# Order of work at the ends of the FFN passes, of banks and of side sums in a one-core Mamba-2 / Conformer trunk

## The chip, the cores and the metric

The kernel runs on one core of a Trainium2 chip. Its time is the device time of one launch in microseconds (us). Five engines run their own queues side by side: TensorE (PE in the profile, its weight loads PEld), VectorE (DVE), ScalarE (ACT), GpSimd (POOL) and SyncE (SP), which issues the loads and stores. An engine takes its instructions in the order of its queue and waits on semaphores for what others produce.

## The reference

A trunk of two residual layers over a sequence of 1024 rows, width D = 1024, float32:

```python
for i in range(DEPTH):                      # DEPTH = 2
    if i == 0: h = h + mamba2_mixer(rmsnorm(h, ssm_norm), ...)
    else:      h = h + conformer_conv_module(rmsnorm(h, cv_norm), ...)
    h = h + (silu(u @ w_gate) * (u @ w_up)) @ w_down      # u = rmsnorm(h, ffn_norm[i]), D_FF = 2816
return rmsnorm(h, final_norm)
```

The mixer is a Mamba-2 layer (input projection, a convolution of 4 taps, a chunked scan over 32 heads, gated norm, output projection). The Conformer module is a product to 2048 columns (pw1) with a sigmoid gate, a causal depthwise convolution of 31 taps, a layer norm over D with silu, and a product back to 1024 columns (pw2).

## The kernel before

Everything is held transposed: features on the 128 partitions, sequence along the free axis, in two blocks of T = 512 columns (block 0 and block 1). h is kept in eight tiles of 128x512 per block. D_FF is 22 tiles of 128 features.

*Products.* Each float32 operand is split into a high and a low part: ScalarE makes the high one (L210), VectorE or GpSimd subtracts to get the low one (L211). `gemm` (L231) then issues three matmuls per pair, low weights first (wlo with uhi, whi with ulo, whi with uhi), all on line L235. A product over D is thus 24 matmuls of 128x512. What a norm yields is called u: `norm_u` multiplies h by the inverse root (L321, tile `un` or `ru`), and splits it into `uhi` and `ulo`.

*FFN.* `ffn` yields, for a part of so many tiles, gate and up products (hidden tiles `hid`), and eight down products `dn`, one per tile of h, with three matmuls per hidden tile of the part: a part of six tiles has 18 matmuls per down product, one of two has 6. After each down product VectorE adds it to h (L870); in the last part of a pass it also adds the square of h to a running sum `ssum` for the next norm (`sq_add`, L256). `rstd_a` splits that sum into `sumh` and `suml`; `rstd_b` sums it over the partitions with two matmuls against ones (L282), and forms the inverse root with ScalarE (L286) and three passes of VectorE in PSUM (L287 to L289). Most gate and up products go through `seven` instead: two tiles of features at once, with both halves of the block, by seven products of half-size operands (matmuls of 128x256, L766) in place of eight. It needs sums of weights (`ws`, `wh`) and sums of u, made by `sums_u`: two `join`s per four feature tiles put uhi + ulo back into a buffer `ru` (L684), then differences (L696 to L698, L704) and splits into `tu`. All of these are 128x1024 passes on VectorE.

*The order.* `run` builds one list of units; `put` and `at` slide side work into places of that list (negative places count from its end). Each engine's queue follows this list, with priorities: the convolution (`conv31`, 8 x 31 VectorE passes, L980) has its priority put back, so that VectorE takes it up where it has nothing else. `chain` and `chain7` string the parts of a pass together; in `chain7` the down products of a part are mixed in among the next part's products, `hold` of them are held back, and those of the last part come at the end. The sequence from the first FFN on is: FFN0 of block 0; the Conformer module of block 0, into which 14 of the 22 tiles of FFN0 of block 1 are woven (their gate and up products stand ahead of pw1 and beside the convolution, their down products cover the layer norm); the other 8 tiles of FFN0 of block 1; the Conformer module of block 1, with 14 tiles of FFN1 of block 0; the other 8 of these; FFN1 of block 1 with the final norm.

*Buffers.* `Slots` gives out named SBUF buffers, longest free first. PSUM has eight banks, given out in turn by `bank`; each new phase (`banks`) begins its turn at the first of its list. A product waits until its bank's last reader is done: for a gate product this is ScalarE's silu (`sg_s`, L834), then VectorE's product with the up half (L835).

*Start.* `selects` (L170) makes two constants for the scan, a selector `sel` and a mask `part`, with fills and affine selections on GpSimd, and one sum on VectorE (L186). It is in the list behind the first norm.

*End.* `final` makes the last norm, in one unit for eight multiplications (L1066) with their stores.

Of the kernel before, what the change touches and what calls it, by code (L numbers as in the profile page):

```python
# [14 lines left out]
P = 128  # L15
# [33 lines left out]
class Slots:  # L49
# [5 lines left out]

    def new(self, name, dt=F32):
        assert self.free, [x[2] for x in self.own.values()]
        i = self.free.popleft()
        self.cnt += 1
        t = self.pool.tile(self.shape, dt, tag=f"{self.prefix}{i}", name=f"{name}_{self.prefix}{self.cnt}")  # L60
        self.own[id(t)] = (i, t, name)
        return t
# [42 lines left out]
class Trunk:  # L105
    def __init__(self, ctx, tc, io):
        self.tc, self.nc, self.io = tc, tc.nc, io
        self.cp = ctx.enter_context(tc.tile_pool(name="cp", bufs=1))
        self.wp = ctx.enter_context(tc.tile_pool(name="wp", bufs=1))
        self.ps = ctx.enter_context(tc.tile_pool(name="ps", bufs=1, space=PSUM))  # L110
        self.banks(mm=(0, 1, 2, 3), ss=(4, 5, 6, 7))
# [25 lines left out]
    def consts(self):  # L137
# [30 lines left out]
        nc.vector.tensor_copy(self.gtr, gt)  # L168
        self.small.drop(tmp)
    def selects(self):  # L170
        nc = self.nc


        tmp = [self.small.new("selo"), self.small.new("selp")]
        nc.gpsimd.memset(self.part, 1.0)
        for k, t in enumerate(tmp):
            selo = t.rearrange("h (q c) -> h q c", c=64)
            nc.gpsimd.memset(t, 1.0)
            for g in range(NG):
                s = selo[32 * g:32 * g + 16]  # L180
                nc.gpsimd.affine_select(out=s, in_=s, pattern=[[1, 8], [0, 64]], compare_op=ALU.is_equal,
                                        fill=0.0, base=8 * k, channel_multiplier=-1)
                m = self.part[32 * g:32 * g + 16, k:k + 1]
                nc.gpsimd.affine_select(out=m, in_=m, pattern=[[0, 1]], compare_op=ALU.is_ge,
                                        fill=0.0, base=-8 * k + 7 * (1 - k), channel_multiplier=2 * k - 1)
        nc.vector.tensor_tensor(self.sel, tmp[0].rearrange("h (q c) -> h q c", c=64),  # L186
                                tmp[1].rearrange("h (q c) -> h q c", c=64), ALU.add)
        self.small.drop(*tmp)
    def halves(self):
# [478 lines left out]

    def sums_u(self, b):

# [8 lines left out]
        def join(q):  # L679
            if q == 0:  # L680
                self.RU[b] = [self.big.new("ru"), self.big.new("ru")]
            h, l = self.UB[b][2 * q:2 * q + 2]
            for j in (slice(0, 2), slice(2, 4)):
                tt(self.RU[b][q][:, j], f32(h[:, j]), f32(l[:, j]), ALU.add)  # L684
# [367 lines left out]
    def final(self, b, part=()):  # L1052
# [8 lines left out]

        def second():
            bc = self.rstd_b(st["x"], D, w=n)
            for d in range(KD):
                h = self.hv(b)[d][:, t0:t0 + n]
                nc.vector.scalar_tensor_tensor(h, h, self.pcol("final", d), bc, op0=ALU.mult, op1=ALU.mult)  # L1066
                nc.sync.dma_start(self.io["yT"][d, :, b * T + t0:b * T + t0 + n], h)
        return [Unit(first), Unit(second)]


    def run(self):
# [20 lines left out]
        dt[0].load = early[0].load = None  # L1092
        q = dt[:1] + nu + early + [call(lambda: self.big.drop(*rb))] + [call(self.selects)] + dt[1:] + ip[:NR]
        q += [call(lambda: self.small.drop(fac))] + ip[NR:]
# [31 lines left out]
        q += cv[4:] + put(c[2:], *at(ln, (-10, -9, -8, -6, -4, -3, -2, -1)))  # L1126
# [4 lines left out]
        q += [call(self.phase7)] + put(c, *at(n0, (-13, -11, -9, -7, -5))) + [call(self.phase, 8)]  # L1131
# [3 lines left out]
        q += put(c[:2], *at(n1, (0, 1))) + [call(self.phase, 6, nc.gpsimd)]  # L1135
# [3 lines left out]
        q += cv[4:] + put(c[2:], *at(ln, (-10, -9, -8, -6, -4, -3, -2, -1)))  # L1139
        q += [call(self.phase, 8)]  # L1140
        self.whole = {1}
        q += put(p2, *at(self.sums_u(0), (2, 3, 4, 5, 6)))
# [110 lines left out]
```

## Time and profile before

| | us |
|---|---|
| median of 3 runs | 2559.18 (2556.84 to 2560.3) |
| the profiled execution, its own time | 2561.22 |
| its span in the trace | 2559.3 |
| TensorE busy | 2502.3 (98%) |
| VectorE busy | 2050.1 (80%) |
| ScalarE busy | 1281.8 (50%) |
| GpSimd busy | 490.6 (19%) |

The span goes from the first to the last instruction; 1.9 us of the launch lie around it. A busy share of a whole span says little about a stage, so the profile is read by windows: for a stretch of time each row gives the busy time of each engine, the count of its instructions in brackets, and PEclk, the mean clock granted to TensorE as a share of full speed.

### The profile page before, as it was taken

How to read it: one execution, taken by the hardware profiler on the slowest of the kernel's cores; microseconds unless marked ns; L12 is line 12 of the kernel's file. 1: busy time of each engine (PE TensorE's matmuls, PEld its weight loads, DVE VectorE, ACT ScalarE, POOL GpSimd, SP SyncE). 2: the span in 40 equal slices, each digit the busy share in tenths (PEclk: the TensorE clock that was granted, in tenths of full speed). 3: DMA queues.
4: the chain of work that ended last, by engine and by line, in shares of the span. 5: the costliest groups of instructions: out<-in, count | busy, mean ns of one | idle time of the engine just before them, and what ended most of it. 6: DMA issues, size and time to landing. Idle time of an engine off the chain costs nothing.

```text
span 2559.3 us, 35509 instructions
## 1 busy us (share of the span) xinstructions
PE 2502.3 (98%) x13570; PEld 2117.2 (83%) x13570; DVE 2050.1 (80%) x2991; ACT 1281.8 (50%) x2284; POOL 490.6 (19%) x466
## 2 busy tenths in 40 slices
PE   8999999999999999997999999989999999999998
PEld 5888787887887799996888889968888899799997
DVE  7888989888888886767899677579996776996675
ACT  5665575666566454444332365352323654554443
POOL 4213312112111000000444530004444300000000
PEclk9999999999999999998999999999999999999999
DMA  4222222222223232222323232222233322332322
GB/s 138 83 71 79 75 63 80 74 78 78 76 70 103 79 122 93 98 73 66 99 94 96 91 132 95 71 75 98 94 97 96 127 99 77 126 122 93 110 89 71
DMA packets 72314, 233.51 MB, mean 91 GB/s; under 512 B 8016, under 2 KB 14416, under 8 KB 65232
## 3 DMA queue, kind: packets, MB, share of 16 engines
q1 hardware_dynamic: 72144, 231.25, 27.9%
q8 instruction: 106, 1.74, 0.3%
q14 instruction: 64, 0.52, 0.1%
HBM read 227.02 MB, written 4.19 MB: 90 GB/s over the span
## 4 chain that ended last, share of the span: by engine, by line
PE 92%; DVE 5%; ACT 1%; DMA 1%; issue 1%; POOL 1%; SPq 0%; DVEq 0%; ACTq 0%; POOLq 0%
PE p L235 65%; PE p L766 21%; PE p L603 1%; PE p L607 1%; DVE wlo L211 1%; PE p L595 1%; PE p L570 1%; PE p L558 1%; DMA wst<-w_dn 1%; PE p L571 1%; DVE h L1066 0%; DVE un_s L321 0%; PE p L586 0%; ACT whi L210 0%; PE p L282 0%
## 5 line engine op out<-in xcount | busy, mean ns | idle before, releaser
L210 ACT ACTIVATE whi<-wst 128x512 fp32r<-128x512 f32 (+3 forms) x676 | 402.7, 597 | 750.4 <-PE p L235 614.2
L235 PE MATMUL p<-uhi_b,wlo 128*128 128x512 f32 x1432 | 574.6, 402 | 20.0 <-ACT sg_s L834 15.1
L235 PE MATMUL p<-ulo_b,whi 128*128 128x512 f32 x1432 | 565.8, 395 | 5.6 <-POOL ulo_b L211 5.5
L235 PE MATMUL p<-uhi_b,whi 128*128 128x512 f32 x1432 | 565.2, 395 | 0.0
L211 POOL TENSOR_TENSOR wlo<-wst,whi 128x512 fp32r<-128x512 f32 x232 | 302.0, 1303 | 775.2 <-ACT whi L210 775.2
L235 PE MATMUL p<-hid_b,whi 128*128 128x512 f32 x1344 | 421.8, 395 | 0.0
L211 DVE TENSOR_TENSOR wlo<-wst,whi 128x512 fp32r<-128x512 f32 (+2 forms) x444 | 306.3, 692 | 141.3 <-ACT whi L210 138.4
L235 PEld LDWEIGHTS p<-uhi_b,wlo 128*128 128x128 f32 x1432 | 271.0, 189 | 87.2 <-ACT sg_s L834 16.1
L235 PEld LDWEIGHTS p<-ulo_b,whi 128*128 128x128 f32 x1432 | 271.0, 189 | 70.6 <-POOL ulo_b L211 7.5
L766 PE MATMUL p<-uhi_b,wh_b 128*128 128x256 f32 x1728 | 322.6, 282 | 1.6 <-ACT uhi_b L210 1.2
L235 PEld LDWEIGHTS p<-uhi_b,whi 128*128 128x128 f32 x1432 | 270.9, 189 | 62.5 <-issue 0.3
L235 PEld LDWEIGHTS p<-hid_b,whi 128*128 128x128 f32 x1344 | 254.1, 189 | 55.6 <-DVE hid_b L211 0.2
L766 PEld LDWEIGHTS p<-uhi_b,wh_b 128*128 128x128 f32 x1728 | 272.6, 189 | 4.3 <-ACT uhi_b L210 1.4
L235 PE MATMUL p<-hid_b,wlo 128*128 128x512 f32 x672 | 266.9, 398 | 6.9 <-DVE h L870 5.2
L766 PE MATMUL p<-ulo_b,wh_b 128*128 128x256 f32 x864 | 243.4, 282 | 0.8 <-DVE ulo_b L211 0.8
L766 PE MATMUL p<-tu_b,wh_b 128*128 128x256 f32 x1296 | 171.4, 282 | 0.0
L766 PEld LDWEIGHTS p<-ulo_b,wh_b 128*128 128x128 f32 x864 | 163.8, 190 | 2.9 <-DVE ulo_b L211 1.0
L766 PEld LDWEIGHTS p<-tu_b,wh_b 128*128 128x128 f32 x1296 | 162.3, 190 | 0.9
L980 DVE SCALAR_TENSOR_TENSOR p<-ci_b,par,p 128x503 f32<-128x503 f32 (+28 forms) x240 | 160.1, 734 | 0.6
L982 DVE SCALAR_TENSOR_TENSOR p<-ci_b,par,p 128x512 f32<-128x512 f32 x232 | 158.7, 750 | 0.5
L210 ACT ACTIVATE wh_b<-ws_b 128x1024 fp32r<-128x1024 f32 x108 | 113.8, 1058 | 86.4 <-PE p L766 35.3
L235 PEld LDWEIGHTS p<-hid_b,wlo 128*128 128x128 f32 x672 | 127.1, 189 | 35.8 <-DVE h L870 7.0
(239 smaller groups left out, 3966.6 us busy)
## 6 DMA issues: line engine op xcount, KB each, us to landing
wq_b<-w_gu SPq DMA_DIRECT2D x54, 1024.0 KB, 4.8
wst<-w_in SPq DMA_DIRECT2D x80, 512.0 KB, 3.5
wst<-w_gu SPq DMA_DIRECT2D x68, 512.0 KB, 3.5
wst<-w_pw SPq DMA_DIRECT2D x48, 512.0 KB, 3.5
wst<-w_dn SPq DMA_DIRECT2D x48, 384.0 KB, 3.2
wst<-w_out SPq DMA_DIRECT2D x64, 256.0 KB, 2.6
wst<-w_dn SPq DMA_DIRECT2D x32, 448.0 KB, 3.3
wst<-w_dn SPq DMA_DIRECT2D x32, 256.0 KB, 2.7
```

What stands on the lines that cost most here:

```text
L210: self.nc.scalar.activation(hi, src, AF.Copy)
L211: (eng or self.nc.vector).tensor_tensor(lo, src, hi.bitcast(F32), ALU.subtract)
L235: self.nc.tensor.matmul(acc, a, b, start=n == 0, stop=n == tot - 1)
L558: nc.tensor.transpose(xt[:, zs(j)], self.XS[i][:, j, zs(z)], self.ident)
L570: nc.tensor.matmul(sg, self.gtr, aml, start=True, stop=False)
L571: nc.tensor.matmul(sg, self.gtr, amh, start=False, stop=True)
L595: nc.tensor.matmul(O[:, zs(j)], H[:, zs(j)], CT[:, zs(z)], start=True, stop=True)
L603: nc.tensor.matmul(Y[po:po + 64, zs(hh // 2)], self.XDT[z % 2][:, hh * 64:(hh + 1) * 64], E[:, zs(r)], start=True, stop=True)
L607: nc.tensor.matmul(S, self.BTOK[:, zs(z)], self.XDD[z % 2], start=True, stop=True)
L766: nc.tensor.matmul(to, x, y, start=n == 0 and not more, stop=n == 11, skip_group_check=True)
L980: nc.vector.scalar_tensor_tensor(acc[:, s:], x[:, HALO:TW - s], w(s), acc[:, s:], op0=ALU.mult, op1=ALU.add)
L982: nc.vector.scalar_tensor_tensor(acc if s < 30 else c, x[:, HALO - s:TW - s], w(s), acc, op0=ALU.mult, op1=ALU.add)
```

## The change

Six edits, all of order, buffers or of who makes a constant; the matmuls and their operands stay what they are.

1. **Parts.** FFN0 of block 0 has parts of 6, 6 and 6 tiles behind the four that the mixer's end has done (6, 6, 4 and 2 before). The pieces of 8 tiles in FFN0's and FFN1's other calls of `chain7` are 2 then 6 (6 then 2 before). `hold` is 0 there, and the other block's norm stands at other places.
2. **Four products ahead.** Of the gate and up products that are woven into a Conformer stage, four stand ahead of pw1 (two before), with the norm's second half behind the first of them; correspondingly two fewer come later.
3. **Banks by age.** A new phase begins its turn at the bank that was taken longest ago.
4. **Selector.** `selects` forms both constants from the identity with eight small VectorE operations, and is called among the first things of the program. GpSimd's 16 selections and 3 fills are gone.
5. **Sums of u.** In the two stages that overlap pw2, `sums_u` takes the buffers that were freed last, not those longest free.
6. **Final scaling.** `final` gives its eight multiplications in four units of two.

```diff
-    def new(self, name, dt=F32):
+    def new(self, name, dt=F32, last=False):
-        i = self.free.popleft()
+        i = self.free.pop() if last else self.free.popleft()
...
     def banks(self, **use):
-        self.use, self.turn = use, dict.fromkeys(use, 0)
+        self.use, self.turn = use, {}
+        for k, b in use.items():
+            self.turn[k] = min(range(len(b)), key=lambda i: self.taken[b[i]], default=0)
     def bank(self, tag):
...
         self.turn[tag] += 1
+        self.count += 1
+        self.taken[i] = self.count
...
     def selects(self):
-        nc.gpsimd.memset(self.part, 1.0)
-        for k, t in enumerate(tmp):
...
+        tt(rows, idg(0), idg(1), ALU.add)
+        tt(rows, rows, idg(2), ALU.add)
+        tt(rows, rows, idg(3), ALU.add)
+        tt(one[:, 0], rows[:, 0], rows[:, 1], ALU.add)
+        for w in (4, 2):
+            tt(rows[:, :, :w], rows[:, :, :w], rows[:, :, w:2 * w], ALU.add)
+        tt(self.part.unsqueeze(2), rows[:, :, 0:1], rows[:, :, 1:2], ALU.add)
+        nc.vector.tensor_copy(self.sel, one[:, 0].unsqueeze(2).to_broadcast([P, 8, 64]))
...
-    def sums_u(self, b):
+    def sums_u(self, b, late=False):
-                self.RU[b] = [self.big.new("ru"), self.big.new("ru")]
+                self.RU[b] = [self.big.new("ru", last=late) for _ in range(2)]
...
-        return [Unit(first), Unit(second)]
+        return [Unit(first)] + [Unit(lambda d=d: second(d)) for d in range(0, KD, 2)]
...
     def run(self):
         self.consts()
+        self.selects()
...
-        c = self.chain7(fast(0, 0, 6, [0]), fast(0, 6, 6, [0]), fast(0, 12, 4, [0]), fast(0, 16, 2, [0], [0]), free=0, hold=5)
-        q += [call(self.phase7)] + put(c, *at(n1, (-11, -9, -7, -5, -3))) + [call(self.phase, 8)]
+        c = self.chain7(fast(0, 0, 6, [0]), fast(0, 6, 6, [0]), fast(0, 12, 6, [0], [0]), free=0, hold=0)
+        q += [call(self.phase7)] + put(c, *at(n1, (-10, -8, -7, -6, -5))) + [call(self.phase, 8)]
...
-        q += put(c[:2], *at(n0, (0, 1))) + [call(self.phase, 6, nc.gpsimd)]
+        q += put(c[:4], *at(n0, (0, 1))) + [call(self.phase, 6, nc.gpsimd)]
...
-        q += put(p2, *at(self.sums_u(1), (2, 3, 4, 5, 6)))
+        q += put(p2, *at(self.sums_u(1, True), (2, 3, 4, 5, 6)))
-        c = self.chain7(fast(0, 0, 6, [1]), fast(0, 6, 2, [1], [1]), free=1, hold=6)
+        c = self.chain7(fast(0, 0, 2, [1]), fast(0, 2, 6, [1], [1]), free=1, hold=0)
...
-        c = self.chain7(fast(1, 14, 6, [0]), fast(1, 20, 2, [0], [0]), free=0, hold=5)
-        q += [call(self.phase7)] + put(c, *at(n1, (-13, -11, -9, -7, -5)))
+        c = self.chain7(fast(1, 14, 2, [0]), fast(1, 16, 6, [0], [0]), free=0, hold=0)
+        q += [call(self.phase7)] + put(c, *at(n1, (-10, -8, -7, -6, -5)))
...
-        q += put(c, *at(self.sums_u(1), (1, 2, 4)), (2, f0[:1]), (3, f0[1:]), (-7, f1[:1]), (-5, f1[1:])) + f2
+        q += put(c, *at(self.sums_u(1), (1, 2, 4)), (2, f0[:1]), (3, f0[1:]), *at(f1, (-7, -5, -4, -3, -2))) + f2
```

Helper lines stand lower in the new file by six or seven: L235 is L241, L211 is L217, L282 is L288, L684 is L691, L766 is L773, L870 is L877, L980 is L987, L1066 is L1075.

How the queues change is seen in three places. The first is TensorE's queue behind the mixer, where four gate and up products follow each other (p_1007, p_1013 and p_1017 are their accumulators, given out in that order, wlo and whi the parts of their weights). Before:

```order
L235 MATMUL p_1007_7430<-ulo_b_7075,whi_7369 128x512
L235 MATMUL p_1007_7430<-uhi_b_7074,whi_7369 128x512
L235 MATMUL p_1017_7502<-uhi_b_6951,wlo_7464 128x512
L235 MATMUL p_1017_7502<-ulo_b_6952,whi_7463 128x512
L235 MATMUL p_1017_7502<-uhi_b_6951,whi_7463 128x512
...
L235 MATMUL p_1013_7471<-uhi_b_6951,wlo_7423 128x512
L235 MATMUL p_1013_7471<-ulo_b_6952,whi_7422 128x512
```

Now:

```order
L241 MATMUL p_1007_7417<-ulo_b_7062,whi_7356 128x512
L241 MATMUL p_1007_7417<-uhi_b_7061,whi_7356 128x512
L241 MATMUL p_1013_7458<-uhi_b_6938,wlo_7410 128x512
L241 MATMUL p_1013_7458<-ulo_b_6939,whi_7409 128x512
L241 MATMUL p_1013_7458<-uhi_b_6938,whi_7409 128x512
...
L241 MATMUL p_1017_7489<-uhi_b_6938,wlo_7451 128x512
L241 MATMUL p_1017_7489<-ulo_b_6939,whi_7450 128x512
```

Nine matmuls of p_1017 stood ahead of p_1013; now p_1013 goes whole ahead of p_1017.

The second is TensorE's queue at the end of FFN0 of block 0: down products (hid), gate and up products of the other block (uhi, ulo), the norm's two matmuls (suml, sumh) and the first of pw1, which reads the u of that norm. Before:

```order
L235 MATMUL p_1286_10661<-hid_b_10556,wlo_10620 128x512
L235 MATMUL p_1286_10661<-hid_b_10556,whi_10619 128x512 x2
...
L235 MATMUL p_1322_10835<-uhi_b_10631,wlo_10803 128x512
...
L235 MATMUL p_1329_10914<-uhi_b_10631,wlo_10824 128x512
...
L282 MATMUL p_1328_10870<-suml_s_10832,onesr 128x512
L282 MATMUL p_1328_10870<-sumh_s_10831,onesr 128x512
L235 MATMUL p_1335_10955<-uhi_b_10878,wlo_10863 128x512
```

Now:

```order
L241 MATMUL p_1300_10753<-hid_b_9974,wlo_10713 128x512
L241 MATMUL p_1300_10753<-hid_b_10289,wlo_10713 128x512
L241 MATMUL p_1300_10753<-hid_b_10475,wlo_10717 128x512
...
L241 MATMUL p_1306_10790<-uhi_b_10486,wlo_10746 128x512
...
L288 MATMUL p_1312_10825<-suml_s_10787,onesr 128x512
L288 MATMUL p_1312_10825<-sumh_s_10786,onesr 128x512
L241 MATMUL p_1313_10869<-uhi_b_10486,wlo_10779 128x512
...
L241 MATMUL p_1331_10985<-uhi_b_10833,wlo_10938 128x512
```

A down product there read one buffer of hidden tiles, six matmuls, and now reads three, 18 matmuls. Pw1's first matmul followed right behind the norm's two, and now follows three whole products behind them.

The third is VectorE's queue, and the joins of u in the Conformer stage of block 0. Before:

```order
L980 SCALAR_TENSOR_TENSOR p_1438_11783<-ci_b_11594,par,p_1438_11783 128x500
L684 TENSOR_TENSOR ru_b_13492<-uhi_b_10631,ulo_b_10632 128x1024
L1002 TENSOR_TENSOR msum_s_12986<-msum_s_12986,co_b_11683 128x512
L870 TENSOR_TENSOR h_762<-h_762,p_1565_12576 128x512
L980 SCALAR_TENSOR_TENSOR p_1438_11783<-ci_b_11594,par,p_1438_11783 128x499
L684 TENSOR_TENSOR ru_b_13492<-uhi_b_10631,ulo_b_10632 128x1024
```

Now:

```order
L217 TENSOR_TENSOR ll_b_13287<-co_b_11713,lh_b_13286 128x512 x2
L691 TENSOR_TENSOR ru_b_13448<-uhi_b_10570,ulo_b_10571 128x1024
L217 TENSOR_TENSOR ll_b_13287<-co_b_11713,lh_b_13286 128x512 x2
L877 TENSOR_TENSOR h_749<-h_749,p_1671_13337 128x512
L691 TENSOR_TENSOR ru_b_13447<-uhi_b_10486,ulo_b_10487 128x1024
L217 TENSOR_TENSOR wlo_13401<-wst_13398,whi_13400 128x512
L691 TENSOR_TENSOR ru_b_13447<-uhi_b_10486,ulo_b_10487 128x1024
```

The joins stood among the last passes of the convolution (L980, and msum, its sum over the tiles), and now stand among the splits of the layer norm's output (ll) and of pw2's weights (wlo).

More of the change, by code (lines that the diff above doesn't have):

```diff
@@ L110, in __init__ @@
         self.ps = ctx.enter_context(tc.tile_pool(name="ps", bufs=1, space=PSUM))
+        self.taken, self.count = dict.fromkeys(range(8), 0), 0
         self.banks(mm=(0, 1, 2, 3), ss=(4, 5, 6, 7))
@@ L171, in selects @@
         nc = self.nc
-        tmp = [self.small.new("selo"), self.small.new("selp")]
-        nc.gpsimd.memset(self.part, 1.0)
-        for k, t in enumerate(tmp):
[L177 to L188, printed above, removed]
+        tt = nc.vector.tensor_tensor
+        t = self.small.new("sels")
+        rows, one = (t[:, 16 * i:16 * i + 16].rearrange("p (k h) -> p k h", k=2) for i in range(2))
+        idg = lambda g: self.ident[:, 32 * g:32 * g + 16].rearrange("p (k h) -> p k h", k=2)
+        tt(rows, idg(0), idg(1), ALU.add)
[6 more added lines that the diff above has]
+        nc.vector.tensor_copy(self.sel, one[:, 0].unsqueeze(2).to_broadcast([P, 8, 64]))
+        self.small.drop(t)
     def halves(self):
@@ L1060, in first, with second @@
             st["x"] = self.rstd_a(("h", b) + part, whole=bool(part))
-        def second():
-            bc = self.rstd_b(st["x"], D, w=n)
-            for d in range(KD):
+        def second(d0):
+            if d0 == 0:
+                st["bc"] = self.rstd_b(st["x"], D, w=n)
+            bc = st["bc"]
+            for d in range(d0, d0 + 2):
                 h = self.hv(b)[d][:, t0:t0 + n]
@@ L1092, in run @@
         dt[0].load = early[0].load = None
-        q = dt[:1] + nu + early + [call(lambda: self.big.drop(*rb))] + [call(self.selects)] + dt[1:] + ip[:NR]
+        q = dt[:1] + nu + early + [call(lambda: self.big.drop(*rb))] + dt[1:] + ip[:NR]
         q += [call(lambda: self.small.drop(fac))] + ip[NR:]
@@ L1125, in run @@
         ln, p2 = self.cnorm(0), self.pw2(0)
-        q += cv[4:] + put(c[2:], *at(ln, (-10, -9, -8, -6, -4, -3, -2, -1)))
+        q += cv[4:] + put(c[4:], *at(ln, (-10, -9, -8, -6, -4, -3, -2, -1)))
         q += [call(self.phase, 8)]
-        q += put(p2, *at(self.sums_u(1), (2, 3, 4, 5, 6)))
+        q += put(p2, *at(self.sums_u(1, True), (2, 3, 4, 5, 6)))
         n0 = self.norm_u(0, "ffn_norm", 8)
-        c = self.chain7(fast(0, 0, 6, [1]), fast(0, 6, 2, [1], [1]), free=1, hold=6)
-        q += [call(self.phase7)] + put(c, *at(n0, (-13, -11, -9, -7, -5))) + [call(self.phase, 8)]
+        c = self.chain7(fast(0, 0, 2, [1]), fast(0, 2, 6, [1], [1]), free=1, hold=0)
+        q += [call(self.phase7)] + put(c, *at(n0, (-10, -8, -7, -6, -5))) + [call(self.phase, 8)]
         n1 = self.norm_u(1, "cv_norm")
@@ L1134, in run @@
         c = self.chain(self.ffn(1, 0, 7, [0]), self.ffn(1, 7, 7, [0]))
-        q += put(c[:2], *at(n1, (0, 1))) + [call(self.phase, 6, nc.gpsimd)]
+        q += put(c[:4], *at(n1, (0, 1))) + [call(self.phase, 6, nc.gpsimd)]
         for j in range(8):
```

4 lines of the change are left out of this document (2 added, 2 removed).

## The prediction

> **What bounds the kernel now.** I read the page's head first, then the chain, then TensorE's waits.
>
> ```profile
> span 2559.3 us, 35509 instructions
> PE 2502.3 (98%) x13570; PEld 2117.2 (83%) x13570; DVE 2050.1 (80%) x2991; ACT 1281.8 (50%) x2284; POOL 490.6 (19%) x466
> PE 92%; DVE 5%; ACT 1%; DMA 1%; issue 1%; POOL 1%; SPq 0%; DVEq 0%; ACTq 0%; POOLq 0%
> PE p L235 <- ACT sg_s L834: 15.1, 2, 7.7
> PE p L235 <- POOL ulo_b L211: 5.5, 4, 2.8
> ```
>
> TensorE is busy for 98% and makes 92% of the chain, and the change leaves its matmuls as they are: it only orders them anew. So all it can win is time in which TensorE stands still or runs below full clock. A view by windows places that time:
>
> ```profile
> core 0: us, PE busy (x) PEld busy (x) DVE busy (x) ACT busy (x) POOL busy (x), PEclk, DMA share, GB/s
> 820.00:860.00 40.00, 37.54 (x156) 29.98 (x155) 35.66 (x49) 22.31 (x34) 0.00 (x0) 0.96 0.26 78
> 1160.00:1220.00 60.00, 46.66 (x177) 36.35 (x176) 44.51 (x73) 31.24 (x51) 4.90 (x4) 0.83 0.22 73
> 1264.00:1324.00 60.00, 60.00 (x262) 48.87 (x261) 55.01 (x86) 20.40 (x33) 28.55 (x27) 1.00 0.29 97
> 1680.00:1720.00 40.00, 30.13 (x114) 23.31 (x113) 32.76 (x54) 21.66 (x36) 1.74 (x2) 0.87 0.27 86
> 2180.00:2240.00 60.00, 54.67 (x264) 45.09 (x263) 55.68 (x84) 34.19 (x58) 0.00 (x0) 0.94 0.38 131
> 2260.00:2300.00 40.00, 40.00 (x339) 40.00 (x338) 35.13 (x48) 21.50 (x34) 0.00 (x0) 1.00 0.32 116
> ```
>
> In the undisturbed 1264:1324, 262 matmuls take 60 us: 0.229 each (128x512). In 2260:2300, 339 of half that width take 40: 0.118. What a window has beyond count times price is lost. 820:860: 40 − 156×0.229 = 4.3. 1160:1220: 60 − 177×0.229 = 19.5. 1680:1720: 40 − 114×0.229 = 13.9. In 2180:2240, 86 of the 264 are half-width, by these rows of the view by form:
>
> ```profile
> L766 PE MATMUL p<-uhi_b,wh_b 128*128 128x256 f32 x41 | 8.4, 288 | 1.2 <-ACT uhi_b L210 1.2
> L766 PE MATMUL p<-ulo_b,wh_b 128*128 128x256 f32 x21 | 6.1, 293 | 0.8 <-DVE ulo_b L211 0.8
> L766 PE MATMUL p<-tu_b,wh_b 128*128 128x256 f32 x24 | 3.2, 282 | 0.0
> ```
>
> 60 − 178×0.229 − 86×0.118 = 9.1. These four places, which I call B, C, E and F, lose 46.8 us together. C, E and F are the ends of three FFN passes. Their loss is more than idle time; TensorE's timeline in C:
>
> ```profile
> 1168.50 0.61 PE L235 MATMUL p<-hid_b,whi 128*128 128x512 f32 x2
> 1169.18 0.61 PE L235 MATMUL p<-hid_b,whi 128*128 128x512 f32 x2
> 1173.96 0.80 PE L235 MATMUL p<-hid_b,wlo 128*128 128x512 f32 x1 [3.49 <-DVE h L870]
> 1174.56 1.05 PE L235 MATMUL p<-hid_b,whi 128*128 128x512 f32 x2
> 1175.84 1.05 PE L235 MATMUL p<-hid_b,whi 128*128 128x512 f32 x2
> ```
>
> Three matmuls took 0.68 us before the 3.49 us idle stretch (1168.50 to 1169.18) and 1.28 after it (1174.56 to 1175.84): a stall of this length is paid for again at half rate. The Trainium skill ("TensorE: Matmul & The Clock Gate", "What's actually happening") puts the half rate down to an idle window of about 3.4 us; the trace agrees with the 1.28 against 0.68.
>
> **The change, part by part.** *B, banks taken by age.* The stall there:
>
> ```profile
> 838.02 0.79 PE L235 MATMUL p<-uhi_b,wlo 128*128 128x512 f32 x1 [2.46 <-DVE wlo L211]
> ```
>
> It is the first matmul of `p_1017`, whose low weights come late, issued ahead of `p_1013`, whose bank was given out later. Now `p_1013`'s 24 matmuls (24×0.229 = 5.5 us) go first, more than the 2.46 that the weights were late. Of 4.3 I take 3.8 as saved (3 to 4.3). No engine gets work for it.
>
> *C and E, six tiles last and four products ahead of the convolution stage.* Now the tail is eight down products with 6 matmuls each from the last two tiles (6×0.229 = 1.4 us), with VectorE owing each an h, a wlo and a sum. Spacing of those, back to back:
>
> ```profile
> 1187.52 0.68 DVE L870 TENSOR_TENSOR h<-h,p 128x512 f32<-128x512 f32 x1
> 1188.12 0.69 DVE L211 TENSOR_TENSOR wlo<-wst,whi 128x512 fp32r<-128x512 f32 x1
> 1188.72 0.68 DVE L870 TENSOR_TENSOR h<-h,p 128x512 f32<-128x512 f32 x1
> 1189.32 0.69 DVE L256 TENSOR_TENSOR ssum_s<-ssum_s,sq_s 128x512 f32<-128x512 f32 x1
> 1198.11 0.70 DVE L288 SCALAR_TENSOR_TENSOR p<-p,rstd_s 128x512 f32<-128x512 f32 x1
> 1203.37 2.72 DVE L321 SCALAR_TENSOR_TENSOR un_s<-h,par,p 128x512 f32<-128x512 f32 x4
> 1206.00 2.49 DVE L211 TENSOR_TENSOR ulo_b<-un_s,uhi_b 128x512 fp32r<-128x512 f32 x4
> ```
>
> 0.60 each, and some 0.34 for a wlo of half the width: at least 1.5 us per 1.4 us of TensorE, and beside it the other block's norm: eight un at 0.66 ((1206.00 − 1203.37)/4) and eight ulo at 0.62 (2.49/4), 10.2 us. VectorE is the bound in the tail. After the change a tail product has 18 matmuls, 4.1 us, eight of them 33.0. VectorE owes 0.60 for h, 0.94 for wlo (four and two tiles) and 0.60 for the sum: 2.14 each, 17.1, and with the norm and its three passes in PSUM (0.70 each, 2.1) 29.4. It fits, with 3.6 to spare. The last h then leads through a square, a sum and a split (0.6 each, with hand-overs about 3.7 us) to the rstd matmul, and one gate product of 24 matmuls (5.5) now stands before that. Three more (16.5) cover VectorE's 2.1 + 10.2, with some 3 us of gating between (five at 0.60): 15.3. The two waits of 15.1 name sg_s: pw1's bank was still held by the silu of the product ahead of it; with four products ahead it is an older one. The price is that the convolution stage has two products fewer as cover before its mean matmul, 11.0 us. I leave 1.5 us of stall in each: C saves 18.0, E 12.4. Without that fit (VectorE late by one norm, 10.2 us, part of it at half rate) either keeps about two thirds of its loss; the upper ends are 19.5 and 13.9.
>
> *F, two tiles first and six last in FFN1.* The same step, but VectorE works 55.68 of 60 us here (93%), with eight final multiplications besides. From the tail to the hidden tile that TensorE next needs, VectorE owes 17.1 for the down products, 12.3 for the norm, 5.3 for the scaling, some 10 for the sums of u (eight passes at 1.22), some 13 for the weights of the next products and 5 for gating: 62. TensorE has 33.0, 22.0 for four products, and 80 half-width matmuls (9.4): 64. Any hand-over of a microsecond shows. I take 3.6 left, 5.5 saved (0 to 8).
>
> *Sums of u behind the convolution.* The joins and sums of `sums_u` leave a stage in which they ran beside the convolution and GpSimd, and go into the 44.0 us of pw2 (8 products of 24).
>
> ```profile
> 1444.00:1474.00 30.00, 30.00 (x130) 23.98 (x129) 6.00 (x7) 11.45 (x21) 15.91 (x13) 1.00 0.32 101
> 1518.00:1563.00 45.00, 45.00 (x196) 36.41 (x195) 32.31 (x41) 20.19 (x30) 2.20 (x2) 1.00 0.37 130
> L684 DVE TENSOR_TENSOR ru_b<-uhi_b,ulo_b 128x1024 f32<-128x1024 f32 x4 | 6.8, 1703 | 0.2 <-PE p L235 0.2
> L684 DVE TENSOR_TENSOR ru_b<-uhi_b,ulo_b x12: 1210/1223/2224, 839.7 to 1930.8; 128x1024 f32<-128x1024 f32 x12
> L210 ACT ACTIVATE wh_b<-ws_b 128x1024 fp32r<-128x1024 f32 x108 | 113.8, 1058 | 86.4 <-PE p L766 35.3
> ```
>
> Where they leave, they take cover from nobody: VectorE has 6.00 us of work in the 30 before the mean matmul, so the convolution was done some 28 us early; minus 11.0 of lost cover, plus at least 8 instructions at 1.70, it still is. Where they go, VectorE's 32.31 gets ten of the twelve 1024-wide passes (two already lie there) at 1.22, the median where GpSimd rests, as it does here (2.20 of 45): 44.5 of 45. They fit by the letter only. A late one would hold the first product of the seven-product scheme. I charge 1 us in each of the two stages (0 to 4). The Trainium skill ("SBUF — State Buffer", "SBUF: two separate sides") has a VectorE operation with two SBUF inputs and GpSimd lock one another out; 1.70 beside GpSimd against 1.22 agrees, and by it the sums lose nothing in pw2.
>
> *Selector by VectorE, at the start.* GpSimd's timeline, and the wait behind it:
>
> ```profile
> 35.82 2.40 POOL L181 TENSOR_SCALAR_AFFINE_SELECT selo_s<-selo_s 16x512 f32<-16x512 f32 x3
> 44.11 1.26 POOL L211 TENSOR_TENSOR ulo_b<-un_s,uhi_b 128x512 fp32r<-128x512 f32 x1
> 46.13 0.69 DVE L186 TENSOR_TENSOR sr_b<-selo_s,selp_s 128x512 fp32r<-128x512 f32 x1 [3.33 <-POOL selp_s L181]
> 19.49 0.74 DVE L339 SCALAR_TENSOR_TENSOR rlo_b<-h,par,rhi_b 128x512 fp32r<-128x512 f32 x1
> 20.15 0.68 DVE L256 TENSOR_TENSOR ssum_s<-ssum_s,sq_s 128x512 f32<-128x512 f32 x1
> ```
>
> Fills and selections push ulo back twice (three of the sixteen: 2.40), and TensorE waited 5.5 for ulo. At best all of it goes, 5.5. VectorE gets seven tiny sums and a copy of 0.6, about 2 us, at a time when its rows stand shoulder to shoulder ahead of the first norm (19.49 to 20.83), so up to 2 us later for everything. I take 2.0 (−2 to 5.5).
>
> *Final scaling in four pieces.*
>
> ```profile
> 2546.77 1.70 PE L235 MATMUL p<-hid_b,wdn_b 128*128 128x256 f32 x12 [0.57 <-DVE h L870]
> 2549.89 0.70 PE L282 MATMUL p<-ssum_s,onesr 128*128 128x256 f32 x2 [1.42 <-DVE ssum_s L256]
> ```
>
> Both waits stand behind eight multiplications queued in one go; in pairs the h and the sum get between them. I take 1.3 of 2.0 (0 to 2.0). Down weights need eight loads fewer on SP's queue; nothing waited there.
>
> Sum: 3.8 + 18.0 + 12.4 + 5.5 − 2.0 + 2.0 + 1.3 = 41.0. The profiled execution took 2561.2 (span 2559.3), 2.0 above the median 2559.2. 2561.2 − 41.0 = 2520.2, and by the median 2518.
>
> **The rivals.** *VectorE becomes the bound where the fit is close.* For it speak 29.4 of 33.0, 62 of 64 and 44.5 of 45; against it that VectorE's busy shares there are below one. Then C and E save 13 and 9, F and the start nothing, pw2 costs 4 in each stage: 3.8 + 13 + 9 − 8 + 1.3 = 19, 2540 by the median. Chance 0.20.
>
> *Slower: the sums stand on the path.* The joins take the buffers freed last, those of the hidden tiles, so they can't begin before the last down product of the stage. If they then run behind pw2's own rows instead of among them, TensorE waits at the entry for twelve passes at 1.22 (14.6), ScalarE's four high halves at about 1.06 (1.22 at most: 4.9), and the first pair's weight sums (about 4): 23 us, some at half rate, twice: 46 to 50. Against the other savings, 43, that gives 2562 to 2566. It decides when VectorE's work in pw2 outruns TensorE's by over 21 us per stage; the 44.5 of 45 says that it doesn't. Chance 0.04.
>
> *No visible gain.* The stalls go elsewhere nearly whole: tails short again behind the four products (VectorE's 15.3 of 16.5), the first rival's costs doubled. Some 3 us of gain are left, 2556. Chance 0.03.
>
> *All closes.* F, startup and entry lose nothing: 4.3 + 19 + 13.5 + 8 + 5 + 2 = 52, 2507. Chance 0.08.
>
> **How the numbers follow.** The forecast has the remaining 0.65. Its own range, from the ends above that don't fall together, is 2511 to 2527. With the first rival and its neighbourhood 2510 to 2541 leaves out about 0.15. A measurement of this kernel tells some 0.2% (5 us) from no change: faster 0.94 (forecast, first rival, all closes, and part of the third case), same 0.03, slower 0.03.
>
> **What would show it.** B: no wait on wlo near 838, `p_1013` before `p_1017`. C and E: windows of 60 us around the last down products with clock 1.00, count × 0.229 within 2 us of their length, no wait of L241 for sg_s. F: 2 to 5 us lost, VectorE above 93%. Pw2: L691 at 1.2 us behind the convolution, VectorE near 45 of 45, and less than 2 us idle before the first L773. Start: no selection on GpSimd, the ulo waits mostly gone. Wrong I would be if L773 waited for tu or wh at the entry, if the tails showed waits for wlo again, or if the first norm came over 2 us late.

## The result, and the profile after

The changed kernel took 2512.37 us (median of 4 runs, 2512.17 to 2513.91), the kernel before 2558.16 (2556.84 to 2560.3, 4 runs beside it). The ratio is 0.9822, with a 95% interval of 0.9805 to 0.9839: some 46 us less. The forecast was 2518, with 2510 to 2541 as its range. The profiled execution took 2513.91 us, 1.7 more than its span, so that the spans, 2559.3 and 2512.2, may be compared: 47.1 us.

The page's head and chain of the changed kernel:

```profile
span 2512.2 us, 35442 instructions
PE 2488.7 (99%) x13570; PEld 2108.8 (84%) x13570; DVE 2038.6 (81%) x2998; ACT 1281.2 (51%) x2284; POOL 466.0 (19%) x439
PE 96%; DVE 3%; ACT 1%; issue 0%; DMA 0%; POOL 0%; SPq 0%; DVEq 0%; ACTq 0%; POOLq 0%
```

TensorE has the same 13570 matmuls as before. Its busy time fell by 13.6 us although its work is the same: matmuls that ran at half rate count as busy longer. Its waits, the longest first (us in total, times, the longest):

```profile
PE p L241 <- DVE rlo_b L345: 3.0, 5, 1.0
PE p L288 <- DVE ssum_s L262: 1.9, 1, 1.9
PE p L241 <- ACT rhi_b L344: 1.6, 1, 1.6
PE p L209 <- DVE onesr L167: 1.5, 1, 1.5
PE p L241 <- ACT uhi_b L216: 1.1, 1, 1.1
PE p L241 <- POOL ulo_b L217: 1.1, 2, 0.9
```

The waits for sg_s (15.1), for h (5.7) and for low weights (5.5) are gone; what is left is the start, waits of 1.0 and less in the mixer (L564, L576), and one wait at the end. The stretches of the four places by windows, with the first pw2 stage and the start:

```profile
core 0: us, PE busy (x) PEld busy (x) DVE busy (x) ACT busy (x) POOL busy (x), PEclk, DMA share, GB/s
816.00:856.00 40.00, 40.00 (x175) 32.46 (x174) 37.12 (x54) 24.45 (x35) 0.00 (x0) 1.00 0.30 91
1146.00:1206.00 60.00, 60.00 (x262) 49.03 (x261) 43.69 (x71) 31.68 (x54) 6.27 (x5) 1.00 0.32 105
1655.00:1700.00 45.00, 45.00 (x197) 36.61 (x196) 28.91 (x45) 22.79 (x37) 6.45 (x5) 1.00 0.32 105
2130.00:2190.00 60.00, 60.00 (x296) 50.08 (x295) 58.34 (x88) 37.59 (x62) 0.00 (x0) 1.00 0.37 121
1495.00:1539.00 44.00, 44.00 (x204) 36.25 (x203) 41.74 (x51) 22.29 (x32) 1.87 (x1) 1.00 0.26 84
30.00:60.00 30.00, 27.23 (x112) 19.71 (x111) 26.77 (x47) 14.92 (x29) 11.59 (x13) 0.94 0.19 65
```

Count times 0.229 gives 40.1 of 40 at B, 60.0 of 60 at C, 45.1 of 45 at E. At F, 75 of the 296 matmuls are half-width: 221×0.229 + 75×0.118 = 59.5 of 60. Nothing is lost at the first three places and half a microsecond at F, where VectorE works 58.34 of 60 us and TensorE still doesn't wait. At the start, in 30:60, TensorE issues 112 matmuls where it issued 94.

### The profile page after: what moved, and what is told of

Same layout as the page of the kernel before. It is cut to its first block, busy times and chain, and to the rows that moved or that the text cites. A ratio compares the mean times of both kernels' runs of the same rounds, so it can differ in the third digit from the quotient of the medians.

```text
span 2512.2 us, 35442 instructions
## 1 busy us (share of the span) xinstructions
PE 2488.7 (99%) x13570; PEld 2108.8 (84%) x13570; DVE 2038.6 (81%) x2998; ACT 1281.2 (51%) x2284; POOL 466.0 (19%) x439
## 4 chain that ended last, share of the span: by engine, by line
PE 96%; DVE 3%; ACT 1%; issue 0%; DMA 0%; POOL 0%; SPq 0%; DVEq 0%; ACTq 0%; POOLq 0%
PE p L241 68%; PE p L773 21%; PE p L609 1%; PE p L613 1%; PE p L601 1%; PE p L576 1%; PE p L564 1%; PE p L577 1%; DVE wlo L217 1%; PE p L592 0%; PE p L288 0%; PE p L544 0%; DVE h L1075 0%; DVE un_s L327 0%; DMA h<-xT 0%
## 5 line engine op out<-in xcount | busy, mean ns | idle before, releaser
L241 PE MATMUL p<-uhi_b,wlo 128*128 128x512 f32 x1432 | 571.6, 399 | 1.3 <-ACT uhi_b L216 1.1
L241 PE MATMUL p<-ulo_b,whi 128*128 128x512 f32 x1432 | 564.4, 394 | 1.2 <-POOL ulo_b L217 1.1
L241 PE MATMUL p<-uhi_b,whi 128*128 128x512 f32 x1432 | 562.7, 393 | 0.0
L217 POOL TENSOR_TENSOR wlo<-wst,whi 128x512 fp32r<-128x512 f32 x224 | 286.0, 1277 | 764.9 <-ACT whi L216 764.8
L241 PE MATMUL p<-hid_b,whi 128*128 128x512 f32 x1344 | 418.6, 393 | 0.0
L217 DVE TENSOR_TENSOR wlo<-wst,whi 128x512 fp32r<-128x512 f32 (+2 forms) x452 | 313.1, 695 | 109.3 <-ACT whi L216 105.7
L241 PEld LDWEIGHTS p<-uhi_b,wlo 128*128 128x128 f32 x1432 | 268.7, 188 | 67.9 <-issue 4.0
L241 PEld LDWEIGHTS p<-ulo_b,whi 128*128 128x128 f32 x1432 | 268.8, 188 | 65.4 <-POOL ulo_b L217 2.8
L773 PE MATMUL p<-uhi_b,wh_b 128*128 128x256 f32 x1728 | 323.3, 282 | 0.0
L241 PEld LDWEIGHTS p<-uhi_b,whi 128*128 128x128 f32 x1432 | 269.0, 188 | 61.9 <-issue 0.3
L241 PEld LDWEIGHTS p<-hid_b,whi 128*128 128x128 f32 x1344 | 252.5, 188 | 55.1
L773 PEld LDWEIGHTS p<-uhi_b,wh_b 128*128 128x128 f32 x1728 | 273.1, 190 | 3.2 <-ACT vw_s L800 0.8
L241 PE MATMUL p<-hid_b,wlo 128*128 128x512 f32 x672 | 264.4, 395 | 0.0
L773 PE MATMUL p<-ulo_b,wh_b 128*128 128x256 f32 x864 | 243.4, 282 | 0.0
L773 PE MATMUL p<-tu_b,wh_b 128*128 128x256 f32 x1296 | 171.6, 282 | 0.0
L773 PEld LDWEIGHTS p<-ulo_b,wh_b 128*128 128x128 f32 x864 | 163.7, 189 | 1.9
L773 PEld LDWEIGHTS p<-tu_b,wh_b 128*128 128x128 f32 x1296 | 162.7, 190 | 1.3
L987 DVE SCALAR_TENSOR_TENSOR p<-ci_b,par,p 128x499 f32<-128x499 f32 (+28 forms) x240 | 160.0, 733 | 0.9
L217 DVE TENSOR_TENSOR wh_b<-ws_b,wh_b 128x1024 fp32r<-128x1024 f32 x108 | 131.3, 1221 | 22.2 <-ACT wh_b L216 21.1
```

The lines of the kernel that those rows point to most:

```text
L217: (eng or self.nc.vector).tensor_tensor(lo, src, hi.bitcast(F32), ALU.subtract)
L241: self.nc.tensor.matmul(acc, a, b, start=n == 0, stop=n == tot - 1)
L773: nc.tensor.matmul(to, x, y, start=n == 0 and not more, stop=n == 11, skip_group_check=True)
L987: nc.vector.scalar_tensor_tensor(acc[:, s:], x[:, HALO:TW - s], w(s), acc[:, s:], op0=ALU.mult, op1=ALU.add)
```

## The experiments

Six kernels undo one edit of the changed kernel each, one adds one edit to the kernel before, two add work to VectorE, and one puts a single stage back. Each was timed beside the kernel before, whose medians in the three sessions were 2559.2, 2559.0 and 2559.1. The changed kernel itself, run again in the second session:

> The changed kernel itself, as the measure for the other runs of this call: 2512, within 2 us. If the place of the sums was what made the run without late sums 2.5 us faster, it lies above 2511 again; if chip or start made it, it comes to 2510.

It took 2513.1 us, ratio 0.9822 (0.9806 to 0.9839).

**Banks from the first of the list again.**

```diff
-        for k, b in use.items():
-            self.turn[k] = min(range(len(b)), key=lambda i: self.taken[b[i]], default=0)
+        self.use, self.turn = use, dict.fromkeys(use, 0)
```

> The changed kernel with each phase beginning its turn of banks at the first of its list again; all else as changed. Theory A (the bank rule matters only behind the mixer): p_1017 comes ahead of p_1013 again and waits about 2.5 us for wlo near 838, with what follows at half rate; some 4 us over the changed kernel (2512), so about 2516, and the ends of the FFN passes stay without loss. Rival (the bank rule is also what took pw1's wait for sg_s away): the two waits of 7 to 8 us come back in front of the convolution stages, 2525 to 2535.

2517.6 us, ratio 0.9837 (0.9822 to 0.9851): 4.6 to 5.3 over the changed kernel, as theory A has it, a little more than its 2516. Its waits have one line of over half a microsecond that the changed kernel hasn't, and TensorE's timeline shows it:

```profile
PE p L239 <- DVE wlo L215: 2.5, 1, 2.5
```

```profile
833.50 0.50 PE L239 MATMUL p<-uhi_b,wlo 128*128 128x512 f32 x1 [2.46 <-DVE wlo L215]
```

No wait for sg_s came back. So the bank rule is needed behind the mixer alone; at C and E the four products do without it.

**Two products ahead instead of four.**

```diff
-        q += put(c[:4], ...)    ...   put(c[4:], ...)
+        q += put(c[:2], ...)    ...   put(c[2:], ...)
```

> The changed kernel with two products ahead of the convolution stages instead of four. Theory A (the four products are the cover of the norm): one product of 5.5 us stands behind the norm's matmuls where VectorE needs about 15, so TensorE waits some 8 to 10 us, part of it repeated at half rate, in front of both convolution stages; 2532 to 2540. Rival (six tiles last already give VectorE the time, and the longer convolution cover gives it back): under 6 us over the changed kernel, below 2518.

2517.4 us, ratio 0.9836 (0.9820 to 0.9853): 4 to 5 over the changed kernel. The rival is right, and theory A, which was the prediction's reasoning, falls. Its wait and the windows around the two ends:

```profile
PE p L241 <- DVE ulo_b L217: 2.0, 4, 0.8
```

```profile
1150.00:1215.00 65.00, 63.99 (x276) 51.29 (x275) 53.33 (x82) 30.57 (x49) 16.51 (x15) 1.00 0.29 95
1655.00:1715.00 60.00, 58.96 (x254) 47.05 (x253) 48.85 (x72) 26.85 (x41) 18.45 (x14) 1.00 0.29 96
```

TensorE waits for one ulo after the other, never over 0.8 us, and keeps its clock of 1.00: 65 − 276×0.229 = 1.8 and 60 − 254×0.229 = 1.8 lost. Pw1's products need the tiles of u one by one, so they run along behind VectorE; the prediction let them wait for all eight.

**Parts, hold and norm places as before.**

```diff
-  fast(0, 12, 6, [0], [0]), free=0, hold=0)        # and norm at -10, -8, -7, -6, -5
+  fast(0, 12, 4, [0]), fast(0, 16, 2, [0], [0]), free=0, hold=5)      # -11, -9, -7, -5, -3
-  fast(0, 0, 2, [1]), fast(0, 2, 6, [1], [1]), free=1, hold=0)
+  fast(0, 0, 6, [1]), fast(0, 6, 2, [1], [1]), free=1, hold=6)       # FFN1 alike
```

> The changed kernel with the parts, hold and the places of the other block's norm as before; four products ahead, banks by age and the rest stay. Theory A (the short tail is a second, separate loss): down products of 6 matmuls at 1.4 us with VectorE at 1.5 each and the norm beside them lose 4 to 7 us at the first two ends, and FFN1 of block 0 loses its 9 again; 2527 to 2536. Rival (the four products alone hid it all): FFN1's end alone comes back, or nothing: 2512 to 2522.

2530.6 us, ratio 0.9886 (0.9872 to 0.9901): 18 over the changed kernel, in theory A's range. Three of its waits and the windows of the three ends:

```profile
PE p L241 <- DVE h L877: 6.4, 3, 3.5
PE p L241 <- ACT uhi_b L216: 3.2, 2, 2.0
PE p L241 <- DVE wlo L217: 2.2, 1, 2.2
```

```profile
1150.00:1215.00 65.00, 59.12 (x246) 46.18 (x245) 50.70 (x83) 36.24 (x60) 7.01 (x6) 0.97 0.28 93
1655.00:1715.00 60.00, 57.44 (x241) 45.95 (x241) 47.02 (x78) 33.13 (x57) 7.71 (x6) 0.97 0.30 99
2150.00:2210.00 60.00, 55.22 (x270) 45.75 (x269) 56.82 (x87) 34.53 (x58) 0.00 (x0) 0.97 0.38 133
```

By the windows C loses 65 − 246×0.229 = 8.7, more than theory A's 4 to 7, and E 60 − 241×0.229 = 4.8. In the third window, FFN1's end, 85 of the 270 matmuls are half-width: 60 − 185×0.229 − 85×0.118 = 7.6. These are 21 us together, 3 more than the run lost: the price of 0.229 is a little too low for some stretches. With short tails TensorE waits for h: VectorE is the bound there, as the prediction said.

**The parts alone, on the kernel before.** The edit is the one above, the other way round.

> The kernel before with the parts, hold and places of the other block's norm as changed, and nothing else: two products ahead, banks from the first of the list, selector on GpSimd, one piece of final scaling, sums in the convolution. Theory A (parts take nearly all of the loss at the three ends, the four products and the banks only some 1 to 4 us each): 38 us less than before, 2519 to 2525. Rival (without younger banks or four products pw1's wait for sg_s stays, 2 x 7.6 us and half clock behind): 2532 to 2540.

2531.3 us, ratio 0.9896 (0.9880 to 0.9913), 28 less than before. Theory A's range was 2519 to 2525, the rival's 2532 to 2540; the measured time lies just below the rival's, since its wait stayed at half its length:

```profile
PE p L235 <- ACT sg_s L834: 6.9, 2, 3.4
```

Two waits of 3.4 in place of 7.5, with a stretch at half rate behind each (the granted clock is 0.97 in 1150:1215 and in 1655:1715). These two runs read together with the two ahead of them: the parts take away the VectorE-bound tails and all of F's loss; the last 5 us each at C and E go by younger banks or by four products, either of them being nearly enough.

**Selector on GpSimd again.**

```diff
-        self.consts()
-        self.selects()          # eight VectorE operations
+        self.consts()           # selects: 16 selections and 3 fills on GpSimd, behind the first norm
```

> The changed kernel with the selector made on GpSimd as before, behind the first norm. Theory A (fills and selections between GpSimd's ulo made TensorE wait): four waits for ulo and half clock near 39 to 49 come back, 3 to 4 us over the changed kernel, 2515 to 2517. Rival (VectorE's part at the start costs as much as it saves): within 1 us, 2511 to 2513.

2517.4 us, ratio 0.9836 (0.9821 to 0.9850): 4.3 over the changed kernel of the same session, at the upper end of theory A's range. The four waits are back in TensorE's list:

```profile
PE p L242 <- POOL ulo_b L218: 4.7, 4, 2.8
```

In the changed kernel GpSimd's timeline has its ulo undisturbed:

```profile
36.03 1.46 POOL L217 TENSOR_TENSOR ulo_b<-un_s,uhi_b 128x512 fp32r<-128x512 f32 x1 [0.24 <-ACT uhi_b L216]
40.10 1.99 POOL L217 TENSOR_TENSOR ulo_b<-un_s,uhi_b 128x512 fp32r<-128x512 f32 x1 [2.60 <-ACT uhi_b L216]
```

The price on VectorE is there as well. The first and second norm's matmuls started at these times, before:

```profile
22.53 0.39 PE L282 MATMUL p<-suml_s,onesr 128*128 128x512 f32 x1
156.29 0.42 PE L282 MATMUL p<-suml_s,onesr 128*128 128x512 f32 x1
```

and after:

```profile
23.94 0.50 PE L288 MATMUL p<-suml_s,onesr 128*128 128x512 f32 x1 [0.52 <-DVE suml_s L217]
153.04 0.41 PE L288 MATMUL p<-suml_s,onesr 128*128 128x512 f32 x1
```

1.4 us later at the first, 3.3 earlier at the second. With the selector on GpSimd the first is early again:

```profile
22.36 0.40 PE L289 MATMUL p<-suml_s,onesr 128*128 128x512 f32 x1
```

**Final scaling in one go.**

```diff
-  ..., *at(f1, (-7, -5, -4, -3, -2))) + f2
+  ..., (-7, f1[:1]), (-5, f1[1:])) + f2
```

> The changed kernel with the eight scaled stores of the last but one half behind one another, as one piece would be. Theory A (the wait for the last sum is a chain of its own, h, square, sum): the wait of 1.9 us at the end stays and a second of 0.6 us comes back; under 1 us over the changed kernel. Rival (the eight multiplications were the cause): 1.5 to 2 us over it.

2513.1 us, ratio 0.9819 (0.9805 to 0.9834), the same as the changed kernel's 2513.1. Its end on TensorE's timeline:

```profile
2498.57 1.68 PE L241 MATMUL p<-hid_b,wdn_b 128*128 128x256 f32 x12 [0.59 <-DVE h L877]
2501.67 0.70 PE L288 MATMUL p<-ssum_s,onesr 128*128 128x256 f32 x2 [1.42 <-DVE ssum_s L262]
```

0.59 and 1.42 here, one wait of 1.9 in the changed kernel: the edit only moves the wait.

**More work for VectorE at FFN1's end.**

```diff
                 nc.vector.tensor_tensor(h, h, acc, ALU.add)
+                if l == 1 and b == 0 and b in done:
+                    for _ in range(2): nc.vector.tensor_tensor(self.dum, h, h, ALU.add)
```

> The changed kernel with two more 128x512 additions of VectorE (h + h into a tile that nobody reads) behind each of the eight last down products of FFN1 of block 0: 16 of 0.60, 9.6 us. Theory A (VectorE has 62 of 64 us there, 2 to spare): TensorE waits 7 us or more, with half clock behind, 2519 to 2524. Rival (the count took in work that VectorE does ahead of time or later, and the true slack is more than 9 us): under 2 us over the changed kernel.

2522.8 us, ratio 0.9858 (0.9844 to 0.9873): 9.7 over the changed kernel for 9.6 of added work. The waits that it adds, and its window:

```profile
PE p L242 <- DVE hid_b L218: 4.2, 1, 4.2
PE p L242 <- DVE h L878: 2.4, 2, 1.2
```

```profile
2140.00:2200.00 60.00, 53.37 (x258) 43.96 (x257) 57.91 (x87) 31.18 (x49) 0.00 (x0) 0.94 0.32 110
```

Theory A is right, but cost and added work are nearly equal by chance. TensorE waits 6.6 us more (4.2 for the hidden tile, 2.4 for h), and the clock of 0.94 over 60 us is another 3.4 or so, two stretches at half rate. So about 3 of the 9.6 us were absorbed; the prediction's 2 to spare was near. VectorE works as much as without the addition (57.91 of 60, 58.34 in the changed kernel's window): it was nearly full.

**More work for VectorE in pw2.**

```diff
             nc.vector.scalar_tensor_tensor(h, acc, self.pcol("b_pw2", d), h, op0=ALU.add, op1=ALU.add)
+            for _ in range(2): nc.vector.tensor_tensor(self.dum, h, h, ALU.add)
```

> The changed kernel with two more 128x512 additions of VectorE (h + h into a tile that nobody reads) behind each of the eight pw2 products in both stages: 9.6 us each. Theory A (VectorE owes 44.5 of 45 there, half a microsecond to spare): 8 to 10 us per stage, 2528 to 2533. Rival (VectorE's idle time before pw2 and the products behind it give slack): under 3 us per stage, below 2519.

2515.0 us, ratio 0.9832 (0.9817 to 0.9847): 2 to 3 over the changed kernel for 19.2 of added work, as the rival has it. Its wait and the stage:

```profile
PE p L774 <- DVE wh_b L218: 1.6, 2, 0.9
```

```profile
1495.00:1539.00 44.00, 43.62 (x206) 35.91 (x204) 44.00 (x59) 20.62 (x29) 0.00 (x0) 1.00 0.26 89
```

VectorE works all 44.00 us here, with 59 instructions in place of 51. By its timeline 14 of the stage's 16 additions start in this window, so some six other instructions are pushed past 1539, into the seven-product stage, and TensorE waits only 0.7 to 0.9 us for wh. The theory that 44.5 of 45 leaves half a microsecond is wrong.

**Late sums undone, in both stages and in one.**

```diff
-        q += put(p2, *at(self.sums_u(1, True), (2, 3, 4, 5, 6)))
+        q += put(p2, *at(self.sums_u(1), (2, 3, 4, 5, 6)))         # sums_u(0) alike
```

> The changed kernel with sums_u taking the longest free buffers again, so that the joins run among the convolution and GpSimd's work. Theory A (there was slack of 28 us less 11 on either side, so the place of the sums is free): within 2 us of the changed kernel, 2510 to 2515, with joins at 1.7 us instead of 1.2. Rival (without the late sums the convolution, with 11 us less cover, ends late at the mean matmul): a wait at L1014 of several us in both stages, 2517 or more.

2509.9 us, ratio 0.9806 (0.9792 to 0.9821): just under theory A's range, and less than the changed kernel. TensorE's queue is the same, instruction by instruction. The joins cost more, by the view of their line, without late sums and with them:

```profile
L691 DVE TENSOR_TENSOR ru_b<-uhi_b,ulo_b x12: 1210/1398/2174, 836.6 to 1900.7; 128x1024 f32<-128x1024 f32 x12
```

```profile
L691 DVE TENSOR_TENSOR ru_b<-uhi_b,ulo_b x12: 1209/1218/2155, 837.0 to 1991.6; 128x1024 f32<-128x1024 f32 x12
```

A median of 1398 against 1218 ns, off the path; with late sums a join takes up to 2155 ns still. Run again, and with the second stage alone put back:

> The changed kernel without late sums once more. It gave 2509.9 where the changed kernel gave 2512.4 and 2513.1, with TensorE's queue the same instruction by instruction. Theory A (the place of the buffers makes matmuls some 0.5% closer between 1680 and 1760 and behind 2170): it repeats, 2509 to 2511. Rival (that was the chip or the start of those runs): 2511.5 to 2514.

> The changed kernel with late sums in the first of the two stages and not in the second. Theory A (what counts is which buffers are in use): the stretch from 1666 to 1939 is as in the changed kernel, and what it gains lies behind 2170, 1 to 2 us; 2510 to 2512. Rival (the sums of the second stage beside the convolution save time there): the gain lies between 1900 and 2120.

2510.2 us, ratio 0.9814 (0.9799 to 0.9828), in theory A's range, and 2512.3, 0.9821 (0.9807 to 0.9836), just above its 2510 to 2512. Four marks on TensorE's timeline (the norms' matmuls and the layer norm's mean), first in the changed kernel of the second session:

```profile
1665.95 0.39 PE L288 MATMUL p<-suml_s,onesr 128*128 128x512 f32 x1
1938.92 1.02 PE L1014 MATMUL p<-msum_s,onesr 128*128 128x512 f32 x2
2171.06 0.40 PE L288 MATMUL p<-suml_s,onesr 128*128 128x512 f32 x1
2492.93 0.60 PE L288 MATMUL p<-ssum_s,onesr 128*128 128x256 f32 x2
```

then in the second run without late sums:

```profile
1664.60 0.40 PE L288 MATMUL p<-suml_s,onesr 128*128 128x512 f32 x1
1936.39 1.02 PE L1014 MATMUL p<-msum_s,onesr 128*128 128x512 f32 x2
2168.20 0.40 PE L288 MATMUL p<-suml_s,onesr 128*128 128x512 f32 x1
2488.39 0.60 PE L288 MATMUL p<-ssum_s,onesr 128*128 128x256 f32 x2
```

Between the first two marks the changed kernel takes 272.97 us, the other 271.79: 1.18 less; between the last two 321.87 and 320.19: 1.68 less. The first run without late sums shows 1.18 and 1.59. With only the second stage put back, the first stretch is as in the changed kernel (272.97) and the last one 1.0 shorter. There is no wait in these stretches that differs: the matmuls stand closer by half a per cent, and from 1680 on, more than 150 us behind the first stage's sums and 200 us ahead of the second's. So the time at which the sums run is hardly the cause; what still differs there is which SBUF buffers the tiles lie in, since the list of free ones has been left in another order. That the place is the cause is argued from this, not shown: no run changed the place alone.

The count of TensorE's matmuls in 240 us beside the second convolution tells the same, in the kernel before, in the changed kernel, and in it without late sums (second run):

```profile
1735.00:1975.00 240.00, 240.00 (x1045) 195.71 (x1044) 205.10 (x295) 75.15 (x122) 115.84 (x89) 1.00 0.29 95
1695.00:1935.00 240.00, 240.00 (x1038) 194.71 (x1037) 198.08 (x293) 74.59 (x121) 113.27 (x89) 1.00 0.29 94
1695.00:1935.00 240.00, 240.00 (x1042) 195.30 (x1041) 211.57 (x302) 74.61 (x121) 115.11 (x89) 1.00 0.30 95
```

The kernel before with the parts alone, which has no late sums either, also issues 1042 in such a stretch (1714:1954).

## Why the prediction was right, point by point

The sum was 41.0; the spans differ by 47.1. Term by term, by the same count of matmuls in the windows and by the marks:

| term | forecast saving | measured |
|---|---|---|
| B, banks | 3.8 | 4.3 |
| C | 18.0 | 19.5 |
| E | 12.4 | 13.9 |
| F | 5.5 | 8.6 |
| sums behind the convolution | −2.0 | 0 at the entry; −2.9 by matmuls further apart |
| start | 2.0 | 3.3 |
| end | 1.3 | 0.4 |

Without the −2.9 the measured terms add up to 50.0, and the spans differ by 47.1. The 2.9 is what undoing the late sums gave back (1.18 + 1.68). That it closes the sum to the tenth is chance: it was measured against the changed kernel, and the kernel before stands closer still, with 1045 matmuls in 240 us where the changed kernel has 1038; 7 × 0.229 is 1.6 us there alone, which the term for E leaves out.

- *B* came as worked out: undone, it costs 4.6 to 5.3, by a wait of 2.46 and a stretch at half rate behind it.
- *C and E.* The tails were the VectorE-bound stretch that the prediction described; short tails again at all three ends cost 18, by the windows 8.7 of it at C and 4.8 at E. The residue of 1.5 each was too much: nothing stayed. The reasoning on the four products was wrong in its size. The prediction asked for 15.3 us of VectorE's work behind 16.5 us of cover, as if pw1 needed the whole u. With one product as cover TensorE lost only 1.8 at each end: pw1's matmuls take the tiles of u in order and follow VectorE. What the four products do is let the silu give back the bank, and younger banks do that also. That the terms came out all the same is in part luck: the change has both edits, and either would nearly have done.
- *F.* The step that sized the residue failed. "Any hand-over of a microsecond shows" was put at 3.6; half a microsecond was left, and the 8.6 saved lies above the term's own 0 to 8. The balance itself, 62 of 64, was good (its terms add up to 62.7): of 9.6 us more of VectorE's work about 3 were absorbed. An engine at 97% in front of TensorE did not delay it. That what TensorE needed was ordered ahead of what it did not is the likely reason; no run reversed that order alone.
- *Pw2.* The forecast of 44.5 us in 45 was near in amount (41.74 of 44), but it took all of it as due by the end of pw2. The added 9.6 us per stage cost about one. The due part is less than what runs there. The charge of 2.0 for it was wrong, and the loss that the late sums do bring, 2.9, has another form, which no row of the profile before could show. That the two sizes are close is luck.
- *Start.* Both sides of the term are there: 1.4 later at the first norm for VectorE's eight operations, 4.7 regained behind it. 2.0 was low by 1.3.
- *End.* The eight multiplications were no cause. The wait of 1.9 for the last sum comes from the chain behind the last down product (h, square, sum); with the scaling in one go it is split in 0.59 and 1.42.

The first rival (VectorE becomes the bound where the fit is close) was the nearest to what the probes say of F: VectorE is nearly full there, and some 3 us more would have shown. The slower rival (sums on the path) would have needed VectorE to fall over 21 us behind TensorE in each stage; TensorE waited 0 at the entry, and 0.7 to 0.9 with 9.6 us added.

The best version that was run is the changed kernel without late sums: 2509.9 and 2510.2 us in two sessions, against 2512.4 and 2513.1 with them. The medians' distance is small against the intervals of the ratios (0.9806 and 0.9814 against 0.9822, each to about 0.0015); that it is real rests on the marks of the two traces, which agree to 0.1 us.

## What to carry to other kernels

Where a pass ends, put its longest products last: the side work per product (here an addition, a split and a sum on VectorE) grows little, by the prediction's prices from 1.5 to 2.1 us, while TensorE's time for it grows from 1.4 to 4.1 us. A busy share close to one in front of TensorE is no forecast of a wait: ask for each piece of work by when it is needed, and take what lies behind that date out of the sum; adding known work to the engine measures the slack, once the waits are told apart from the half rate behind them. Several edits can close the same wait, so what each is worth alone must be found by undoing it and by doing it alone: the four undoings that cost anything add up to 32 of the 46 us here.

## What the runs showed of the hardware

Idle stretches well under 3.4 us can cost a stretch at half rate. The gap of 2.46 at B cost 4.3 in all; it stands in three traces (the kernel before, it with the parts alone, the changed kernel with the old bank rule), each time with such a stretch. In the kernel with the old parts, the window 1655:1715 holds one longer wait, the 2.2 for wlo, and a clock of 0.97 of 60 us, which is 1.8 us or one stretch of 3.4 at half rate; 1150:1215 holds two, 3.5 for h and 2.0 for uhi, and its 0.97 of 65 is again one stretch, so that the 2.0 left no trace in the clock. The Trainium skill ("TensorE: Matmul & The Clock Gate", "What's actually happening") names an idle window of about 3.4 us; the length of the half-rate stretch agrees, the idle time that brought it was shorter here.

No limit on the idle time follows from these runs. In the changed kernel's second run and in its first, TensorE's longest wait around 263 us was 1.04 and 0.93 us long, and only the second run had a stretch at half rate there:

```profile
263.00:272.00 9.00, 8.74 (x31) 6.59 (x32) 7.78 (x12) 5.64 (x15) 1.94 (x4) 0.81 0.17 46
263.00:272.00 9.00, 7.95 (x35) 5.77 (x34) 8.87 (x14) 6.54 (x15) 2.77 (x4) 1.00 0.19 60
```

With one and the same queue of matmuls, the spacing of matmuls differed by half a per cent over some hundred microseconds between two kernels whose lists of free buffers stood in another order, 2.9 us in all, without a wait in the profile. What makes the difference is open.
